# First loads on two queues, direct stacking and paired residual loads in a two-layer decoder trunk

## The chip, the cores and the metric

The kernel runs on one core of one Trainium2 chip. The metric is the device time of one execution in microseconds (us), as the median of several runs. The engines are TensorE (PE in the profile; PEld is its weight load), VectorE (DVE), ScalarE (ACT), GpSimd (POOL) and SyncE (SP, which here only issues DMAs). ACT and POOL can issue DMAs as well.

## The reference

Two pre-norm residual layers over 512 positions of width 2048, and a last normalisation. All sizes here are float32.

```python
for layer in range(2):
    h = rmsnorm(x, norm_g[layer])
    parts = split(h @ w_in[layer], 8)           # 8 parts of 256 columns
    if layer % 2 == 0:
        qa, ka, va, ga, qb, kb, vb, gb = parts
        oa = dilated_mixture(rope(heads(qa)), rope(heads(ka)), heads(va))
        ob = moba(rope(heads(qb)), rope(heads(kb)), heads(vb))
        y = concat(merge(oa) * silu(ga), merge(ob) * silu(gb))
    else:
        qc, kc, vc, gc, qd, kd, vd, gd = parts  # q and k of C in two halves of 32
        oc = diff_attention(rope(qc), rope(kc), heads(vc), lam, subln_g)
        od = stick_breaking(heads(qd), heads(kd), heads(vd))
        y = concat(merge(oc) * silu(gc), merge(od) * silu(gd))
    x = x + y @ w_out[layer]                    # y has 512 columns
return rmsnorm(x, final_norm_g)
```

Each of the four branches has 4 heads of 64.

## The kernel before

Every product is made from split operands. An operand a is rounded to a high part (type fp32r) on ACT, and DVE or POOL forms the low part, a minus the high part. A product is then three matmuls: high by high, low by high and high by low (`mm3`, L185). The activations lie transposed, 16 tiles of 128 features by 512 positions: HH and HL are the high and low parts of x times the gain.

The weights come in 80 units of 128x1024 (512 KB), 40 for each layer, in the order of use. `load_unit` (L142) loads a unit into one of three `raw` buffers, and `split_half` (L159) splits half a unit into whi and wlo, of which there are two buffers. `tick` (L178) is called once for each half unit of matmuls; it keeps the loads up to four units and the splits two half units ahead. All these loads stand in SP's queue, which works in program order, as every engine does.

A layer first makes the projections. In layer 0 the values V come first: `v_unit_half` (L314) runs 16 k tiles, each with 12 matmuls of 512 columns for the four blocks of 128 positions. Then 12 chunks of 128 columns (q, k and gates) are made. The work of the heads is put into this stream of matmuls at positions written out by hand (`SCHED`, L41). Chunks of q and k are rotated on DVE and stacked for the score matmuls: high and low parts of one head stand one above the other in the partitions of a tile st, so that one matmul sums several of the three products. For branch C of layer 1, with 32 rows for each half head, `stack4` (L366) does this with DMAs from tiles hi and lo.

The output projection (`outproj`, L635) has 16 chunks dc of 128 features. Each is made of four parts, one for each pair of heads (`part`, L627; 12 matmuls in all), added to the residual xr by `evac`, and in layer 0 written to DRAM as x1d. The first PRE chunks (2 in layer 0, 5 in layer 1) are opened before the last gate's y is there, with three parts each. `get_x` (L616) loads residuals three chunks ahead; in layer 1 into the four buffers of tag "prob", one tile of 512 columns in each buffer of 1280. The accumulators are PSUM banks of tags "acc" (2 banks) and "s" (3 banks). In layer 1 the projection makes 384 of the positions transposed, and `last` (L646) makes the other 128 in their natural layout, also after the projection; the residual is transposed on PE for these (L678). `after` (L657) takes squares for the last normalisation and multiplies by the last gain on ACT (L663); `scale_t` (L702) multiplies by the reciprocal root at the end.

At the start, `run` (L931) issues WARM matmuls of zeros, then the first loads on SP: xg (the first tile of x and the gain columns together), the two halves of unit 0, tile 1 of x, unit 1 and tiles 2 to 4 of x. The first tile's HH and HL are made on DVE (L240, L241).

Of the kernel before, what the change touches and what calls it, by code (L numbers as in the profile page):

```python
# [39 lines left out]
WARM = 8  # L40
# [42 lines left out]
class Body:  # L83
# [58 lines left out]
    def load_unit(self, part=0):  # L142
# [3 lines left out]
        if part == 2:  # L146
            self.nc.sync.dma_start(self.raw[0][:, 512:], self.a["w"][0][:, 512:])
            self.nload += 1
            return
        if part == 1:  # L150
            self.raw[0] = self.wp.tile([128, 1024], F32, tag="raw", bufs=3, name="raw")
            self.nc.sync.dma_start(self.raw[0][:, :512], self.a["w"][0][:, :512])
            return
        self.nload += 1
        t = self.wp.tile([128, 1024], F32, tag="raw", bufs=3, name="raw")
        self.nc.sync.dma_start(t, self.a["w"][u])
# [28 lines left out]
    def mm3(self, out, lh, ll, rh, rl, first, last):  # L185
        mm = self.nc.tensor.matmul
        mm(out, lhsT=lh, rhs=rh, start=first, stop=False)  # L187
        mm(out, lhsT=lh, rhs=rl, start=False, stop=False)  # L188
        mm(out, lhsT=ll, rhs=rh, start=False, stop=last)  # L189
# [44 lines left out]
    def make_h(self, x, l, kt, square=True, g=None):  # L234
        nc = self.nc
        if g is None:
            g = self.g[:, l, kt:kt + 1]
            nc.scalar.activation(self.HH[:, kt], x, AF.Copy, scale=g)
        else:
            nc.vector.tensor_scalar(self.HH[:, kt], x, g, None, op0=OP.mult)  # L240
# [14 lines left out]
    def load_x(self, src, kt, tag=None):  # L255
        if tag:
            x = self.ap.tile([128, 1280], F32, tag=tag, bufs=4, name="xr")[:, :S]
        else:
            x = self.tmp("xr")
        self.nc.sync.dma_start(x, src[kt])  # L260
        return x
# [52 lines left out]
    def v_unit_half(self, u, half, kt):  # L314
        h, l = self.whi[u], self.wlo[u]
        w = slice(512 * half, 512 * half + 512)
        if u == 0 and half == 0:
            for x, y in ((self.HH, h), (self.HL, h), (self.HH, l)):
                for t in range(NT):
                    self.nc.tensor.matmul(self.vps[t], lhsT=x[:, kt, 128 * t:128 * t + 128], rhs=y[:, w],  # L320
                                          start=x is self.HH and y is h, stop=False)
# [44 lines left out]
    def stack4(self, st, src, key):  # L366
# [693 lines left out]
```

## Time and profile before

| | us |
|---|---|
| median of 3 runs | 527.46 (527.19 to 529.7) |
| profiled execution | 527.0 |
| its span, first to last instruction | 524.9 |
| PE busy | 511.5 (97%) |
| DVE busy | 331.8 (63%) |
| ACT busy | 293.3 (56%) |
| POOL busy | 180.0 (34%) |

The profile is of one execution. The page gives busy times and groups; the timeline lists instructions in order of time, and what ended the idle time before one. Matmuls are pipelined: in the timeline a matmul's drawn duration overlaps the next one's.

### The profile page before, as it was taken

The numbers are of one execution on the slowest core, as the hardware profiler recorded it, in microseconds if no ns is written. First come the engines' busy times: TensorE is split into PE (matmuls) and PEld (weight loads), VectorE is DVE, ScalarE is ACT, GpSimd is POOL, SyncE is SP. The second block draws the span as 40 slices with busy tenths as digits, with TensorE's granted clock in tenths as the row PEclk, the third lists the DMA queues.
The fourth block names the chain that finished last, engine by engine and source line by source line (L and its number), as shares of the span: only waits on it lengthen the run. The fifth ranks groups of instructions, "written<-read, shape, count | busy, mean of one in ns | idle before, by whom it ended". The sixth has DMA issues, their size and how long they took to land.

```text
span 524.9 us, 7398 instructions
## 1 busy us (share of the span) xinstructions
PE 511.5 (97%) x2505; PEld 430.7 (82%) x2505; DVE 331.8 (63%) x678; ACT 293.3 (56%) x588; POOL 180.0 (34%) x171
## 2 busy tenths in 40 slices
PE   8999999999999999999999998999999999999993
PEld 5888888888888888788888887888888888898993
DVE  5545358787786755797862872564557856784444
ACT  5477244355436554566546464743446678857843
POOL 2304353304224023377403233114520322444841
PEclk9999999999999999999999999999999999999998
DMA  8895352244314223688534274232551313156717
GB/s 306 282 401 180 120 124 93 68 117 121 120 41 121 81 80 107 204 288 302 182 121 121 80 200 123 83 119 80 146 145 71 108 54 116 62 179 208 239 70 252
DMA packets 30374, 77.65 MB, mean 148 GB/s; under 512 B 4480, under 2 KB 7424, under 8 KB 29952
## 3 DMA queue, kind: packets, MB, share of 16 engines
q1 hardware_dynamic: 27264, 70.36, 39.3%
q0 software_dynamic: 2784, 6.29, 5.5%
q10 hardware_dynamic: 288, 0.52, 0.3%
q8 instruction: 20, 0.33, 0.3%
q14 instruction: 18, 0.15, 0.1%
HBM read 61.43 MB, written 8.39 MB: 133 GB/s over the span
## 4 chain that ended last, share of the span: by engine, by line
PE 91%; DMA 3%; ACT 2%; DVE 2%; issue 1%; POOL 0%; ACTq 0%; SPq 0%; POOLq 0%
PE acc L187 17%; PE acc L189 17%; PE acc L188 17%; PE oacc L188 5%; PE oacc L189 5%; PE oacc L187 5%; PE v L187 4%; PE v L189 4%; PE v L188 4%; PE ops L509 3%; PE pt L481 3%; PE s L415 2%; DMA st<-st 1%; PE z L532 1%; PE s L446 1%
## 5 line engine op out<-in xcount | busy, mean ns | idle before, releaser
L176 POOL TENSOR_TENSOR wlo<-raw,whi 128x512 fp32r<-128x512 f32 x67 | 90.7, 1359 | 192.3 <-ACT whi L174 146.9
L187 PE MATMUL acc<-hh,whi 128*128 128x512 f32 x384 | 154.2, 402 | 0.0
L189 PE MATMUL acc<-hh,wlo 128*128 128x512 f32 x384 | 150.1, 391 | 0.0
L188 PE MATMUL acc<-hl,whi 128*128 128x512 f32 x384 | 149.7, 390 | 0.0
L174 ACT ACTIVATE whi<-raw 128x512 fp32r<-128x512 f32 x148 | 90.5, 625 | 88.7 <-issue 42.7
L189 PEld LDWEIGHTS acc<-hh,wlo 128*128 128x128 f32 x384 | 72.1, 188 | 15.6
L188 PEld LDWEIGHTS acc<-hl,whi 128*128 128x128 f32 x384 | 72.3, 188 | 12.9
L187 PEld LDWEIGHTS acc<-hh,whi 128*128 128x128 f32 x384 | 72.3, 188 | 12.7
L176 DVE TENSOR_TENSOR wlo<-raw,whi 128x512 fp32r<-128x512 f32 x81 | 59.2, 737 | 29.4 <-ACT whi L174 26.9
L187 PE MATMUL v<-whi,hh 128*128 128x512 f32 x124 | 48.4, 390 | 0.0
L189 PE MATMUL v<-whi,hl 128*128 128x512 f32 x124 | 48.3, 389 | 0.0
L188 PE MATMUL v<-wlo,hh 128*128 128x512 f32 x124 | 48.2, 389 | 0.0
L395 ACT ACTIVATE prob<-prob,m 128x512 f32<-128x512 f32 (+3 forms) x56 | 29.7, 552 | 28.3 <-DVE m L392 28.3
L487 DVE TENSOR_TENSOR pt<-pt 128x384 fp32r<-128x384 f32 (+1 forms) x48 | 27.4, 598 | 22.2 <-ACT pt L486 22.1
L486 ACT ACTIVATE pt<-pt 128x384 fp32r<-128x384 f32 (+1 forms) x48 | 23.5, 524 | 27.2 <-PE pt L481 26.9
L187 PE MATMUL oacc<-y,whi 128*128 128x512 f32 (+1 forms) x80 | 30.9, 386 | 0.1
L188 PE MATMUL oacc<-y,whi 128*128 128x512 f32 (+1 forms) x80 | 30.4, 380 | 0.2 <-DVE y L577 0.2
L189 PE MATMUL oacc<-y,wlo 128*128 128x512 f32 (+1 forms) x80 | 30.3, 378 | 0.0
L189 PEld LDWEIGHTS v<-whi,hl 128*128 128x128 f32 x124 | 23.3, 188 | 4.9
L188 PEld LDWEIGHTS v<-wlo,hh 128*128 128x128 f32 x124 | 23.3, 188 | 4.7
L187 PEld LDWEIGHTS v<-whi,hh 128*128 128x128 f32 x124 | 23.3, 188 | 4.6
L253 POOL TENSOR_TENSOR ss<-ss,sq 128x512 f32<-128x512 f32 x15 | 21.8, 1451 | 11.2 <-ACT sq L249 11.1
(219 smaller groups left out, 836.8 us busy)
## 6 DMA issues: line engine op xcount, KB each, us to landing
raw<-w SPq DMA_DIRECT2D x79, 512.0 KB, 3.4
xr<-xt SPq DMA_DIRECT2D x31, 256.0 KB, 4.4
xnat<-xnat SPq DMA_DIRECT2D x8, 512.0 KB, 7.5
x1d<-x SPq DMA_DIRECT2D x16, 256.0 KB, 2.8
xr<-x1d SPq DMA_DIRECT2D x16, 256.0 KB, 3.5
st<-st POOLq DMA_DIRECT2D x24, 128.0 KB, 3.5
out_t_dram<-x2a SPq DMA_DIRECT2D x10, 192.0 KB, 2.8
out_t_dram<-x2b SPq DMA_DIRECT2D x6, 192.0 KB, 2.5
```

The costliest lines, as they stand in the source:

```text
L174: self.nc.scalar.activation(h, t, AF.Copy)
L176: eng.tensor_tensor(l, t, h.bitcast(F32), op=OP.subtract)
L187: mm(out, lhsT=lh, rhs=rh, start=first, stop=False)
L188: mm(out, lhsT=lh, rhs=rl, start=False, stop=False)
L189: mm(out, lhsT=ll, rhs=rh, start=False, stop=last)
L253: nc.gpsimd.tensor_tensor(ss, ss, sq, op=OP.add)
L395: nc.scalar.activation(p, p, AF.Exp, bias=m[:, t:t + 1], scale=-1.0, **kw)
L415: nc.tensor.matmul(out, lhsT=Q()[:, 2 * i + arr, 128 * t:128 * t + 128], rhs=Q()[:, 4 + i, :n], start=arr == 0, stop=arr == 1)
L481: nc.tensor.transpose(bank[:, col + 128 * (t - c):col + 128 * (t - c) + 128], st["p"][:, QOFF[t] + 128 * c:QOFF[t] + 128 * c + 128], self. ...
L486: nc.scalar.activation(h, src, AF.Copy)
L487: nc.vector.tensor_tensor(l, src, h.bitcast(F32), op=OP.subtract)
L509: nc.tensor.matmul(b[:, 128 * c:], lhsT=self.V[:, c, vh], rhs=st[k][:, OFF[c]:OFF[c] + WID[c]], start=c == 0 and k == "h", stop=c == NT - ...
```

## The change

At the start, the first half of unit 0 is issued from ACT's queue, and xg is cut in two, half of the first tile with the gains first. ACT issues unit 1, unit 2 and tiles 2 to 4 of x between its first splits. The first tile's HH and HL are made in halves, and the first twelve matmuls go through the first two position blocks before the others. There are seven warm matmuls in place of eight. In `stack4` every copy is made straight from hi and lo: eight transfers of 64 KB on SP and eight on POOL, where four and four were followed by copies from the stacked tile to itself. In the output projections, the two first chunks do the two matmuls that don't need the last gate's low part before the third; in layer 0 the chunks 2 to 4 also take banks of tag "s". In layer 1 residuals are loaded in pairs. The last gain of chunks 0 to 4 moves from ACT into the final scaling.

```diff
-WARM = 8
+WARM = 7
...
-    def load_unit(self, part=0):
+    def load_unit(self, part=0, eng=None):
...
-        self.nc.sync.dma_start(t, self.a["w"][u])
+        (eng or self.nc.sync).dma_start(t, self.a["w"][u])
...
+    def mm3(self, out, lh, ll, rh, rl, first, last, which=3):
         mm = self.nc.tensor.matmul
+        if which == 3:
+            mm(out, lhsT=lh, rhs=rh, start=first, stop=False)
+            mm(out, lhsT=lh, rhs=rl, start=False, stop=False)
+            mm(out, lhsT=ll, rhs=rh, start=False, stop=last)
+        elif which == 2:
+            mm(out, lhsT=lh, rhs=rh, start=first, stop=False)
+            mm(out, lhsT=ll, rhs=rh, start=False, stop=False)
+        else:
+            mm(out, lhsT=lh, rhs=rl, start=False, stop=last)
...
+    def make_h0(self, i):
+        nc = self.nc
+        o = i * (S // 2 + 3 * KT)
+        x, g = self.xg[:, o:o + S // 2], self.xg[:, S // 2:S // 2 + 1]
+        w = slice(S // 2 * i, S // 2 * i + S // 2)
+        nc.vector.tensor_scalar(self.HH[:, 0, w], x, g, None, op0=OP.mult)
+        nc.vector.scalar_tensor_tensor(self.HL[:, 0, w], x, g, self.HH[:, 0, w].bitcast(F32),
+                                       op0=OP.mult, op1=OP.subtract)
...
         if u == 0 and half == 0:
-            for x, y in ((self.HH, h), (self.HL, h), (self.HH, l)):
-                for t in range(NT):
+            for x, y, t in [(x, y, t) for ts in ((0, 1), (2, 3))
+                            for x, y in ((self.HH, h), (self.HL, h), (self.HH, l)) for t in ts]:
...
+        hrows, lrows = ((0, 96), (32, 64)) if key else ((0, 64), (32, 96))
         for i in range(4):
             p = slice(32 * i, 32 * i + 32)
-            nc.sync.dma_start(sf[0:32, z + i], hi[p])
-            nc.gpsimd.dma_start(sf[32:64, z + i], lo[p])
-        if key:
-            nc.gpsimd.dma_start(sf[64:96, z:z + 4], sf[32:64, z:z + 4])
-            nc.gpsimd.dma_start(sf[96:128, z:z + 4], sf[0:32, z:z + 4])
-        else:
-            nc.gpsimd.dma_start(sf[64:128, z:z + 4], sf[0:64, z:z + 4])
+            for k in range(2):
+                nc.sync.dma_start(sf[hrows[k]:hrows[k] + 32, z + i], hi[p])
+                nc.gpsimd.dma_start(sf[lrows[k]:lrows[k] + 32, z + i], lo[p])
...
+    def get_pair(self, k):
+        if k < KT // 2:
+            t = self.ap.tile([128, 1280], F32, tag="prob", bufs=4, name="xr")[:, :2 * S]
+            t = t.rearrange("p (k s) -> p k s", k=2)
+            self.nc.sync.dma_start(t, self.px[2 * k:2 * k + 2].rearrange("k p s -> p k s"))
+            self.xs[2 * k], self.xs[2 * k + 1] = t[:, 0], t[:, 1]
...
             for k in range(3):
-                self.get_x(k)
-        self.accs[dc] = self.bank("acc" if dc < 2 or dc >= PRE[self.pl] else "s", "oacc")[:, :self.pw]
+                self.get_pair(k) if self.pl else self.get_x(k)
+        self.accs[dc] = self.bank("s" if 2 <= dc < 5 else "acc", "oacc")[:, :self.pw]
...
         for dc in range(KT):
-            self.get_x(dc + 3)
-            if dc < PRE[self.pl]:
+            if not self.pl:
+                self.get_x(dc + 3)
+            elif dc % 2 == 0:
+                self.get_pair(dc // 2 + 3)
+            if dc < 2:
+                if dc == 0:
+                    self.part(0, 3, 2)
+                    self.part(1, 3, 2)
+                self.part(dc, 3, 1)
+            elif dc < PRE[self.pl]:
                 self.part(dc, 3)
...
-            nc.scalar.activation(X[dc], X[dc], AF.Copy, scale=self.g[:, 2, dc:dc + 1])
+            if dc >= PRE[1]:
+                nc.scalar.activation(X[dc], X[dc], AF.Copy, scale=self.g[:, 2, dc:dc + 1])
...
-                eng.tensor_tensor(X[dc], X[dc], r, op=OP.mult)
+                if dc < PRE[1]:
+                    eng.scalar_tensor_tensor(X[dc], X[dc], self.g[:, 2, dc:dc + 1], r, op0=OP.mult, op1=OP.mult)
+                else:
+                    eng.tensor_tensor(X[dc], X[dc], r, op=OP.mult)
...
                 if kt == 0:
-                    self.make_h(self.x0.pop(0), 0, 0, False, self.xg[:, S:S + 1])
+                    q = self.nc.scalar
+                    self.make_h0(0)
                     self.split_half()
+                    self.load_unit(0, q)
+                    self.x0[2] = self.load_x(self.a["xt"], 2, q)
+                    self.make_h0(1)
                     self.split_half()
                     self.make_h(self.x0.pop(1), 0, 1, False)
+                    for k in (3, 4):
+                        self.x0[k] = self.load_x(self.a["xt"], k, q)
+                    self.load_unit(0, q)
...
-        nc.sync.dma_start(self.xg, self.a["xg"])
-        self.x0[0] = self.xg[:, :S]
+        c = S // 2 + 3 * KT
+        nc.sync.dma_start(self.xg[:, :c], self.a["xg"][:, :c])
+        self.load_unit(1, nc.scalar)
+        nc.sync.dma_start(self.xg[:, c:], self.a["xg"][:, c:])
         nc.scalar.preload_act_table_set("exp_and_others")
-        self.load_unit(1)
-        self.load_unit(2)
+        self.load_unit(2, nc.sync)
         self.x0[1] = self.load_x(self.a["xt"], 1)
-        nc.gpsimd.tensor_copy(self.g.rearrange("p a b -> p (a b)"), self.xg[:, S:])
-        self.load_unit()
-        for kt in range(2, 5):
-            self.x0[kt] = self.load_x(self.a["xt"], kt)
+        nc.gpsimd.tensor_copy(self.g.rearrange("p a b -> p (a b)"), self.xg[:, S // 2:c])
```

## Rows read from the trace of the kernel before

**Rows 1.** The page, part 1: busy time, share of the span and instructions.

```profile
PE 511.5 (97%) x2505; PEld 430.7 (82%) x2505; DVE 331.8 (63%) x678; ACT 293.3 (56%) x588; POOL 180.0 (34%) x171
```

**Rows 2.** What PE waited for: total us, times, longest.

```profile
PE s L446 <- DMA st<-st: 1.6, 1, 1.6
...
PE xnp L678 <- DMA xr<-x1d: 0.9, 1, 0.9
```

**Rows 3.** Timeline, start: begin us, duration us, engine, line, operation, count [idle before <-releaser].

```profile
0.74 0.38 SPq L941 DMA_DIRECT2D xg<-xg  x1
...
1.18 0.42 SPq L152 DMA_DIRECT2D raw<-w  x1
...
1.19 3.48 PE L938 MATMUL warm<-zero 128*128 128x512 bf16 x8 [1.19 <-DVE zero L935]
...
3.55 0.53 DVE L240 TENSOR_SCALAR hh<-xg 128x512 fp32r<-128x512 f32 x1 [2.42 <-DMA xg<-xg]
...
4.57 0.63 ACT L174 ACTIVATE whi<-raw 128x512 fp32r<-128x512 f32 x1 [2.55 <-DMA raw<-w]
...
5.25 1.19 PE L320 MATMUL v<-whi,hh 128*128 128x512 f32 x4 [0.58 <-ACT whi L174]
```

**Rows 4.** Timeline, the k tiles behind the first; last, a DMA issue on ACT.

```profile
7.39 0.75 DVE L241 SCALAR_TENSOR_TENSOR hl<-xr,gcols,hh 128x512 fp32r<-128x512 f32 x1 [0.35 <-ACT hh L238]
...
8.03 0.63 ACT L174 ACTIVATE whi<-raw 128x512 fp32r<-128x512 f32 x1 [0.68 <-DMA raw<-w]
8.11 0.39 PE L187 MATMUL v<-whi,hh 128*128 128x512 f32 x1
...
9.45 0.75 DVE L241 SCALAR_TENSOR_TENSOR hl<-xr,gcols,hh 128x512 fp32r<-128x512 f32 x1
9.47 0.39 PE L187 MATMUL v<-whi,hh 128*128 128x512 f32 x1
...
519.12 0.41 ACTq L804 DMA_DIRECT2D out_n_dram<-nat  x1
```

**Rows 5.** Timeline, PE and DVE, where the first output projection closes its first chunks.

```profile
213.98 0.51 PE L187 MATMUL oacc<-y,whi 128*128 128x512 f32 x1
214.70 0.50 PE L188 MATMUL oacc<-y,whi 128*128 128x512 f32 x1 [0.22 <-DVE y L577]
...
215.47 1.39 DVE L958 TENSOR_TENSOR x<-oacc,xr 128x512 f32<-128x512 f32 x2 [0.82 <-PE oacc L189]
...
215.74 0.39 PE L189 MATMUL oacc<-y,wlo 128*128 128x512 f32 x1
216.21 0.50 PE L187 MATMUL oacc<-y,whi 128*128 128x512 f32 x1
...
217.03 0.40 PE L187 MATMUL oacc<-y,whi 128*128 128x512 f32 x1
```

**Rows 6.** Timeline, the second stacking of layer 1 and the scores behind it.

```profile
308.67 2.78 SPq L375 DMA_DIRECT2D st<-hi  x4
...
309.66 1.98 POOL L376 DMA_DIRECT2D st<-lo  x4 [1.96 <-DVE lo L372]
...
319.48 0.63 ACT L174 ACTIVATE whi<-raw 128x512 fp32r<-128x512 f32 x1 [2.89 <-PE v L189]
...
323.02 0.88 PE L446 MATMUL s<-st 128*128 128x512 f32 x4 [1.59 <-DMA st<-st]
```

**Rows 7.** The chain that ended last: begin us, us, what (a DMA until its landing).

```profile
311.14 3.21 DMA st<-lo
...
315.49 7.18 DMA st<-st
...
475.43 2.60 DMA xr<-x1d
```

**Rows 8.** Timeline: a gain on ACT in the second projection; DVE in the tail.

```profile
475.96 0.62 ACT L663 ACTIVATE x2a<-x2a,gcols 128x384 f32<-128x384 f32 x1
...
510.13 0.69 DVE L715 TENSOR_TENSOR nat<-nacc,nat 128x512 f32<-128x512 f32 x1 [0.28 <-PE nacc L189]
```

More of the change, by code (lines that the diff above doesn't have):

```diff
@@ L146, in load_unit @@
         if part == 2:
-            self.nc.sync.dma_start(self.raw[0][:, 512:], self.a["w"][0][:, 512:])
+            eng.dma_start(self.raw[0][:, 512:], self.a["w"][0][:, 512:])
             self.nload += 1
@@ L151, in load_unit @@
             self.raw[0] = self.wp.tile([128, 1024], F32, tag="raw", bufs=3, name="raw")
-            self.nc.sync.dma_start(self.raw[0][:, :512], self.a["w"][0][:, :512])
+            eng.dma_start(self.raw[0][:, :512], self.a["w"][0][:, :512])
             return
@@ L183, in tick @@
         self.gh += 1
-    def mm3(self, out, lh, ll, rh, rl, first, last):
+    def mm3(self, out, lh, ll, rh, rl, first, last, which=3):
         mm = self.nc.tensor.matmul
-        mm(out, lhsT=lh, rhs=rh, start=first, stop=False)
-        mm(out, lhsT=lh, rhs=rl, start=False, stop=False)
-        mm(out, lhsT=ll, rhs=rh, start=False, stop=last)
+        if which == 3:
[7 more added lines that the diff above has]
+            mm(out, lhsT=lh, rhs=rl, start=False, stop=last)
     def rstd(self, ss, n, mul, add=None, eng=None):
@@ L253, in square, with load_x @@
             nc.gpsimd.tensor_tensor(ss, ss, sq, op=OP.add)
[L255 to L260, printed above, removed]
+    def load_x(self, src, kt, eng=None):
+        x = self.tmp("xr")
+        (eng or self.nc.sync).dma_start(x, src[kt])
         return x
@@ L317, in v_unit_half @@
         if u == 0 and half == 0:
-            for x, y in ((self.HH, h), (self.HL, h), (self.HH, l)):
-                for t in range(NT):
-                    self.nc.tensor.matmul(self.vps[t], lhsT=x[:, kt, 128 * t:128 * t + 128], rhs=y[:, w],
-                                          start=x is self.HH and y is h, stop=False)
+            for x, y, t in [(x, y, t) for ts in ((0, 1), (2, 3))
+                            for x, y in ((self.HH, h), (self.HL, h), (self.HH, l)) for t in ts]:
+                self.nc.tensor.matmul(self.vps[t], lhsT=x[:, kt, 128 * t:128 * t + 128], rhs=y[:, w],
+                                      start=x is self.HH and y is h, stop=False)
             return
@@ L623, in open_dc, with part @@
             for k in range(3):
-                self.get_x(k)
-        self.accs[dc] = self.bank("acc" if dc < 2 or dc >= PRE[self.pl] else "s", "oacc")[:, :self.pw]
-    def part(self, dc, j):
+                self.get_pair(k) if self.pl else self.get_x(k)
+        self.accs[dc] = self.bank("s" if 2 <= dc < 5 else "acc", "oacc")[:, :self.pw]
+    def part(self, dc, j, which=3):
         u, k = self.pl * UNITS + 32 + dc // 2, dc % 2
@@ L632, in part @@
         self.mm3(self.accs[dc], h[:, e], lo[:, e], self.YH[:, e, :self.pw], self.YL[:, e, :self.pw],
-                 j == 0, j == 3)
+                 j == 0, j == 3, which)
     def outproj(self, evac):
         for dc in range(KT):
-            self.get_x(dc + 3)
-            if dc < PRE[self.pl]:
+            if not self.pl:
[8 more added lines that the diff above has]
+            elif dc < PRE[self.pl]:
                 self.part(dc, 3)
```

14 lines of the change are left out of this document (6 added, 8 removed).

## The prediction, made before the change was built or run

> **What bounds the kernel now.** I read the page first: PE is busy 97% of the span [rows 1], so no other engine is the bound over any long stretch, and what an edit can win is the time in which PE stands still. Then the list of what PE waited for [rows 2]: it has few entries, and the two on DMAs name one place each. Then, in PE's timeline, the starts of the matmuls. The reader has to know one thing of that view: a 128x512 matmul is drawn 0.39 us long, but the next starts earlier: from 8.11 to 9.47 are six undisturbed steps [rows 4], so 0.227 us each. So an idle time g in the view is a loss of about g + 0.16 us, and a loss is best read from starts. I went through all starts in that way. Beside some 90 ns after each run of transposes, PE loses time in four places: the start, the first output projection, the first s of layer 1 and the second output projection. The change touches all four. After the last matmul stands a tail of DVE, ACT and stores, which it hardly touches.
>
> **The start.** The first real matmul starts at 5.25; it waits for the split on ACT (4.57 to 5.20), which waits for the first half of the first weight tile, issued on SP at 1.18, behind xg at 0.74 [rows 3]. The change issues this half on ACT's queue, so at 0.74, and cuts xg: 152 KB go ahead, 128 KB behind. The landing of two transfers issued at the same time on two queues is not in this trace. Early end: as xg alone, 280 KB from 0.74 to 3.55 [rows 3], so 3.55 instead of 4.55, a gain of 1.0; the seven warm matmuls, 3.48/8 = 0.43 each [rows 3], then end near 4.2 and no longer fit much gain than that. Late end: the two queues share and the half lands as before, gain 0. I take 0.5, in the middle and near the 0.44 us by which the issue comes earlier. The Trainium skill, "DMA: Bandwidth & Descriptors", section "Issuing engines are not separate DMA queues", speaks against more: transfers from several engines interleave on the same DMA engines and a second issuer saves its issue time alone. By it the term would be 0.44; this trace, with one queue in use there, doesn't show it. The half-width HH and HL on DVE (0.53 in full width [rows 3]) come before the split ends, and the new order of the first twelve matmuls needs only these halves for its first six, so they don't set the start.
>
> What is then late next? PE has twelve matmuls per k tile, 2.86 us for the first [rows 3, 4]. The second k tile would start at 4.75 + 2.86 = 7.6 and needs HL of x1 two steps later, at 8.06; it was ready at 7.39 + 0.75 = 8.14 [rows 4]. With the same bytes ahead of x1, a wait of 0.1 at most remains. For the third k tile, ACT now issues five loads among its first splits, 0.41 each [rows 4]: two before the second split, where ACT waited for data anyway, and three, 1.2 us, ahead of the split that stood at 8.03. ACT was idle 0.68 there, so split and HH come about 0.5 later, and PE wants them 0.5 earlier. HL of x2 ended at 9.45 + 0.75 = 10.20, and was wanted at 8.11 + 2.72 + 0.45 = 11.28: of a margin of 1.1, 0.1 is left. So the supply is at the edge but holds; if raw 1 and raw 2, now issued 2 to 3 us later, share the DMA engines with raw 3 and x5 of SP, I bound the loss at 0.8. Range of the start: -0.3 to +1.0, value 0.5.
>
> **The first output projection.** Two chunks stand ready but for the last gate. The first of their last three matmuls starts at 213.98, the second waits for the low part of y (214.70), and the third chunk waits at 215.74 to 216.21 for a PSUM bank, because DVE empties the first chunk only from 215.47 [rows 5]. From 213.98 to 217.03 are nine steps; undisturbed they take 9 x 0.227 = 2.04, here they took 3.05: 1.0 lost. After the change four matmuls that don't need the low part come first, 4 x 0.227 = 0.91, so the low part is wanted at 214.89 and is there at 214.70; chunks 2 to 4 take banks of tag "s", free since the attention heads. Chunks 5 and 6 take "acc" again, over 8 us of PE after these are emptied. Gain 1.0; what could be late next is DVE's evacuation, twelve matmuls (2.7 us) per 0.70 us of DVE. Lower bound 0.6 (the bank alone late), upper 1.0.
>
> **Direct stacking.** For each of four chunks of layer 1, the split halves go from hi and lo to the stacked tile. Before, four 64 KB transfers on SP and four on POOL, then POOL waits for these to land and issues one or two copies of 256 or 512 KB from the tile to itself. The last such copy takes 7.18 us, to 322.67 [rows 7], and s starts at 323.02 after 1.59 us of idle: a loss of 1.75 [rows 6]. After: eight on each queue, the same bytes, no second stage. SP: 308.67 + 8 x 2.78/4 = 314.2; POOL: 309.66 + 8 x 1.98/4 = 313.6 [rows 6]. With the 3.21 us that a first-stage transfer took [rows 7], the last lands near 317.4; even with the 7.18 of the copies it is 321.4, when PE is there at 321.28. So the whole 1.75 is won; lower bound 1.6. What is queued behind: on SP four more issues, 2.8 us, stand before the next weight load (311.55 before). The split that uses that load (319.48) waited for PE, not for the load [rows 6], and it is made at least two half units ahead of its use, 24 matmuls or 5.4 us: the delay is hidden; without that cover it would cost up to 1. On POOL the queue gets free sooner than before (313.6, where the last copy was issued from 315.49 on [rows 7]), so splits behind it gain. The other three stackings had no loss and have none to win.
>
> **Residual pairs.** In the second output projection the fifth residual tile was issued at 475.43, since the four buffers were full until the first chunk was emptied, and landed 2.60 later [rows 7]; PE was idle 0.9 [rows 2], a loss of 0.9 + 0.16, some 1.0. After, a buffer holds two tiles: three pairs are asked for where three tiles were, the fourth pair where the fourth tile was, so tiles 0 to 7 are there before PE reaches the fifth chunk. The same bytes; half the issues on SP. Gain 1.0. What is late next there is ACT: squares, gains and splits follow each other closely, 0.62 us for each gain [rows 8]. The change takes five of these off ACT (chunks 0 to 4, 3.1 us), more than PE gains, so the splits keep their lead. Lower bound 0.5.
>
> **The gains moved to the end.** The five are multiplied in on DVE in the final scaling: a two-operand instruction becomes a three-operand one. Such a pair stands at 0.69 [rows 8] and 0.75 [rows 4] for 512 columns: 0.05 for 384, 0.2 for the first four. They stand before DVE's wait of 0.28 for PE [rows 8], which hides them; uncovered they cost 0.25.
>
> **Sum.** 0.5 + 1.0 + 1.75 + 1.0 = 4.25. The profiled execution took 527.0 (span 524.9 and 2.1 around it), so 522.8. The median of the runs is 527.46, 0.46 more, and gives 523.2. I forecast 523.0. With all terms at their lower ends (-0.3, 0.6, 1.6, 0.5; and 0.25 lost in the tail) the gain is 2.2, the time 525.3 from the median; with all at the upper ends 4.75, 522.3 from the profiled execution.
>
> **Rivals.** (a) The start gives nothing or takes some back: shared DMA engines, or ACT's issues making the third to fifth k tile late. For it: margins of 0.1. Against: each of these was ahead by 1 us before. It gives 523.5 to 524.3. (b) One of the inner stalls is only replaced: s still waits because raw loads and sixteen small transfers share the engines, or the second projection becomes bound by ACT's splits. For: the copies took 7.18 where the first stage took 3.2, so transfers there did get in each other's way. Against: the margins above. It costs 1.0 to 1.75 of the sum: 524.0 to 525.0. (c) Slower than before: TensorE's clock. The warm matmuls run at 0.43 per 512 columns, the 1.2 GHz level; the first real ones, after 0.58 us idle, at 0.23, the 2.4 GHz level [rows 3, 4]. One warm matmul fewer could leave the lower level standing when the real ones begin; each then costs 0.2 more. From 22 such matmuls on (22 x 0.2 = 4.4) it eats the whole sum, from 35 on the kernel is over 0.5% slower, and 40 of them give 523.2 + 8 = 531. Against: the idle time before the first real matmul is about as long as before, so activity hardly changes. The Trainium skill, "TensorE: Matmul & The Clock Gate", Part 1, adds that the moment of release shifts from run to run; one trace can't show that.
>
> **How the numbers follow.** Forecast 0.69, (a) 0.14, (b) 0.12, (c) 0.05. Half a per cent, 2.6 us, is about what a measurement of this kernel can tell from no change: faster means below 524.8. The forecast lies there, but not with every term at its low end; with (a) that is 0.81. Most of (b) at its worst, such a forecast at its low end and (c) in a mild form (20 to 35 matmuls) give same, 0.15; slower 0.04. Range 521.9 to 525.3: up to the sum of the low ends, which takes in (a) and (b) whole; down to the upper ends and 0.4 below, since the lowest run before is 0.3 under the median.
>
> **What would show it.** First real matmul near 4.75 at 0.23 steps; no PE wait on DMA st or xr; nine steps in 2.05 us where the first projection closes; s near 319.8 (323.02 less 0.5, 1.0 and 1.75), with no idle. It would be wrong if PE's gaps among the first five k tiles add up to over 0.5, if the first real matmuls are 0.43 apart, or if s still shows a wait.

## The result, and the profile of the changed kernel

| us | before | after |
|---|---|---|
| median of the runs on the same chip | 528.37 (527.19 to 529.7) | 523.7 (522.72 to 525.54) |
| profiled execution | 527.0 | 524.88 |
| its span | 524.9 | 522.7 |

The ratio is 0.9921, with an interval of 0.9901 to 0.9942: the changed kernel takes 0.8% less time, clear of the interval. The same kernel on another chip gave 0.994 (0.992 to 0.9959), a median of 524.74 (523.11 to 525.47). The 527.46 that the prediction set out from was the median of the first three of the seven runs before. Ratios are worked out over all runs and differ by up to 0.15% from the quotient of the medians. Two runs of the experiments, one of e7 (574.19 us) and one of e10 (2946.32 us), were far slower than all others of their kernels and are left out of medians and ratios. The two profiled executions are only 2.1 us apart, because the one before was faster than all seven timed runs and the one after was the second slowest of its seven. So the profiles can't be subtracted as totals; each stage is read from the starts of its matmuls.

Part 1 of the page (busy us, share of the span, instructions) answers [rows 1]:

```profile
PE 511.6 (98%) x2504; PEld 431.1 (82%) x2504; DVE 335.7 (64%) x680; ACT 289.8 (55%) x583; POOL 187.2 (36%) x181
```

What PE waited for in the changed kernel (line, releaser, us in total, times, longest), beside [rows 2]:

```profile
PE warm L970 <- DVE zero L967: 1.2, 1, 1.2
PE v L188 <- ACT hh L252: 0.6, 1, 0.6
PE v L189 <- POOL wlo L176: 0.2, 1, 0.2
```

Both waits on DMAs, st and xr, are gone, and so is the one on the split in front of the first real matmul (0.58 in [rows 3]; in e12, the same kernel, it was there again with 0.49). Two are new, and both stand in the fifth k tile of the start. The first is on ACT's hh, the second on POOL's wlo.

The start, in PE's timeline of the changed kernel (start, us, engine, line, operation, tiles, count, and in brackets idle time before it with what ended it), beside [rows 3]:

```profile
1.19 3.17 PE L970 MATMUL warm<-zero 128*128 128x512 bf16 x7 [1.19 <-DVE zero L967]
4.51 1.22 PE L329 MATMUL v<-whi,hh 128*128 128x512 f32 x2
5.53 0.86 PE L329 MATMUL v<-whi,hl 128*128 128x512 f32 x2
6.23 0.62 PE L329 MATMUL v<-wlo,hh 128*128 128x512 f32 x2
...
8.05 0.39 PE L188 MATMUL v<-whi,hh 128*128 128x512 f32 x1
```

The first real matmul starts at 4.51 instead of 5.25. But two matmuls take 1.02 (4.51 to 5.53), the next two 0.70, and only from 6.23 on 0.46. Twelve undisturbed steps are 2.72, so the second k tile could have started at 4.51 + 2.72 = 7.23. It starts at 8.05: 0.82 are lost without any idle time, and the second k tile is only 0.06 ahead of that before.

Then the fifth k tile, in the timeline of ACT, POOL and PE:

```profile
15.71 0.63 ACT L174 ACTIVATE whi<-raw 128x512 fp32r<-128x512 f32 x1 [4.28 <-DMA raw<-w]
...
16.25 0.70 ACT L252 ACTIVATE hh<-xr,gcols 128x512 fp32r<-128x512 f32 x1
16.42 1.28 POOL L176 TENSOR_TENSOR wlo<-raw,whi 128x512 fp32r<-128x512 f32 x1 [4.19 <-ACT whi L174]
...
17.01 0.51 PE L188 MATMUL v<-whi,hh 128*128 128x512 f32 x1 [0.59 <-ACT hh L252]
...
17.75 0.49 PE L189 MATMUL v<-wlo,hh 128*128 128x512 f32 x1 [0.24 <-POOL wlo L176]
```

ACT stands idle 4.28 us for a weight load; its split comes at 15.71, its hh at 16.25, and PE waits. The chain of waits that leads there names the load (start, us, what):

```profile
7.56 8.04 DMA raw<-w
```

This is unit 2. ACT issued it at 7.56, as the last of its five loads, and it took 8.04 us to land. Before, in the timeline of SP and ACT:

```profile
4.56 2.83 SPq L156 DMA_DIRECT2D raw<-w  x2
...
11.38 0.63 ACT L174 ACTIVATE whi<-raw 128x512 fp32r<-128x512 f32 x1 [0.83 <-DMA raw<-w]
```

The first of SP's two loads is unit 2: it was issued at 4.56, took 6.7 us to land, and ACT split it from 11.38 on. So of the 4.3 us by which the split now comes later, 3.0 are the later issue and 1.3 the longer landing. The sixth k tile now starts at 20.70 instead of 18.99: at that point the changed kernel is 1.71 us behind. Everything that it wins, it wins later.

The first output projection in PE's timeline, beside [rows 5]:

```profile
215.69 0.50 PE L192 MATMUL oacc<-y,whi 128*128 128x512 f32 x1
216.03 0.39 PE L193 MATMUL oacc<-y,wlo 128*128 128x512 f32 x1
...
216.72 0.63 PE L195 MATMUL oacc<-y,whi 128*128 128x512 f32 x2
217.19 0.39 PE L188 MATMUL oacc<-y,whi 128*128 128x512 f32 x1
```

From 215.69 on, the four matmuls that don't need the low part of y, then the two that do (L195), then the third chunk (217.19). No idle time is left. One step is 0.34 long, the others 0.23.

The stacking of layer 1 beside [rows 6] and [rows 7]: issues on SP and POOL in the timeline, then the table of DMA issues for the stretch from 308 to 323 (KB each, median us to landing), then PE's timeline.

```profile
309.46 5.19 SPq L386 DMA_DIRECT2D st<-hi  x8
...
314.76 1.09 SPq L156 DMA_DIRECT2D raw<-w  x2
...
310.45 3.91 POOL L387 DMA_DIRECT2D st<-lo  x8 [3.51 <-DVE lo L381]
```

```profile
st<-hi SPq DMA_DIRECT2D x8, 64.0 KB, 2.7
st<-lo POOLq DMA_DIRECT2D x8, 64.0 KB, 2.6
```

```profile
321.85 0.39 PE L190 MATMUL v<-whi,hl 128*128 128x512 f32 x1
322.07 0.79 PE L452 MATMUL s<-st 128*128 128x512 f32 x4
```

The last of the eight on SP is issued by 314.65 and lands some 2.7 later; s starts at 322.07, one step after the matmul before it. The copies of the tile to itself, 7.18 us for the last, have left the chain.

The transposes of the fourth and the fifth residual tile in the second projection, in PE's timeline, first before, then after, beside [rows 2] and [rows 7]:

```profile
476.52 0.27 PE L678 MATMUL xnp<-ident,xr 128*128 128x128 f32 x1
...
478.17 0.30 PE L678 MATMUL xnp<-ident,xr 128*128 128x128 f32 x1 [0.86 <-DMA xr<-x1d]
```

```profile
475.39 0.27 PE L700 MATMUL xnp<-ident,xr 128*128 128x128 f32 x1
...
476.02 0.27 PE L700 MATMUL xnp<-ident,xr 128*128 128x128 f32 x1
```

From the fourth to the fifth it was 1.65 and is 0.63; none of the transposes waits any more. And DVE's tail, first before, then after, beside [rows 8]:

```profile
507.90 1.95 DVE L705 TENSOR_TENSOR x2a<-x2a,rep 128x384 f32<-128x384 f32 x4 [0.16 <-ACT R L297]
```

```profile
505.71 2.19 DVE L728 SCALAR_TENSOR_TENSOR x2a<-x2a,gcols,rep 128x384 f32<-128x384 f32 x4 [0.16 <-ACT R L306]
507.95 0.69 DVE L740 TENSOR_TENSOR nat<-nacc,nat 128x512 f32<-128x512 f32 x1
```

The four scalings take 2.19 instead of 1.95, and DVE's wait of 0.28 for PE behind them is gone: the gains cost DVE 0.24, near the 0.2 put in the prediction for the first four, and the end nothing.

From starts at fixed places, the stages of the profiled executions (us, changed kernel less the kernel before): start, to the sixth k tile, +1.71; first projection -0.91; stacking -1.75; second projection -1.06, and another -0.17 between s and its beginning, whose cause was not looked for; tail -0.08. The span: -2.26.

### The profile page after: what moved, and what is told of

Read it like the earlier page. It is cut to its first block, busy times and chain, and to the rows that moved or that the text cites. A ratio compares the mean times of both kernels' runs of the same rounds, so it can differ in the third digit from the quotient of the medians.

```text
span 522.7 us, 7398 instructions
## 1 busy us (share of the span) xinstructions
PE 511.6 (98%) x2504; PEld 431.1 (82%) x2504; DVE 335.7 (64%) x680; ACT 289.8 (55%) x583; POOL 187.2 (36%) x181
## 3 DMA queue, kind: packets, MB, share of 16 engines
q0 software_dynamic: 2944, 5.25, 4.5%
## 4 chain that ended last, share of the span: by engine, by line
PE 94%; DMA 3%; ACT 1%; DVE 1%; SPq 0%; issue 0%; ACTq 0%
PE acc L188 17%; PE acc L190 17%; PE acc L189 17%; PE v L190 5%; PE v L188 5%; PE v L189 5%; PE oacc L188 5%; PE oacc L190 5%; PE oacc L189 5%; PE ops L515 4%; PE pt L487 3%; PE s L421 2%; DMA raw<-w 2%; PE z L538 1%; PE s L452 1%; DMA xr<-xt 1%
## 5 line engine op out<-in xcount | busy, mean ns | idle before, releaser
L190 PEld LDWEIGHTS acc<-hh,wlo 128*128 128x128 f32 x384 | 72.1, 188 | 15.6
L176 DVE TENSOR_TENSOR wlo<-raw,whi 128x512 fp32r<-128x512 f32 x81 | 61.4, 764 | 30.2 <-ACT whi L174 29.5
L188 PE MATMUL oacc<-y,whi 128*128 128x512 f32 (+1 forms) x76 | 29.1, 383 | 0.0
L190 PE MATMUL oacc<-y,wlo 128*128 128x512 f32 (+1 forms) x76 | 28.8, 379 | 0.0
L189 PE MATMUL oacc<-y,whi 128*128 128x512 f32 (+1 forms) x76 | 28.8, 379 | 0.0
L265 POOL TENSOR_TENSOR ss<-ss,sq 128x512 f32<-128x512 f32 x15 | 23.5, 1567 | 8.5 <-ACT sq L261 8.4
```

The costliest lines, as they stand in the source:

```text
L176: eng.tensor_tensor(l, t, h.bitcast(F32), op=OP.subtract)
L265: nc.gpsimd.tensor_tensor(ss, ss, sq, op=OP.add)
```

## The experiments

The questions were where the start's gain had gone, and whether the three inner parts stand on their own. All kernels compute the whole reference. The table gives the median of the runs and the ratio to the kernel before on the same chip (so "before" has one median for each of the four chips), and three places of the one profiled execution; e10 and e11 stand in the text alone. "Lost in k tile 1" is the start of the second k tile less that of the first real matmul less 2.72; "lost to k tile 6" is the start of the sixth less that of the second less 10.88 (four k tiles of 2.72). In e7 a wait of 0.2 for hh is part of the first of these; the second, in e7 and in e3, falls in the second k tile, not in the fifth.

| kernel | median us | ratio (interval) | first real matmul | lost in k tile 1 | lost to k tile 6 | span |
|---|---|---|---|---|---|---|
| before | 526.95 to 528.37 | 1 | 5.25 | 0.14 | 0 | 524.9 |
| after | 523.7 | 0.9921 (0.9901 to 0.9942) | 4.51 | 0.82 | 1.77 | 522.7 |
| after, again (e12) | 524.74 | 0.994 (0.992 to 0.9959) | 4.85 | 1.93 | 0 | 522.4 |
| inner parts alone (e1) | 523.9 | 0.993 (0.9906 to 0.9955) | 5.49 | 0.15 | 0 | 521.4 |
| start alone (e2) | 527.62 | 1.0023 (1.0 to 1.0045) | 4.92 | 0.14 | 0.51 | 525.7 |
| later loads on SP (e3) | 524.61 | 0.9942 (0.9921 to 0.9964) | 4.84 | 0.38 | 0.10 | 520.9 |
| 8 warm (e4) | 523.62 | 0.9929 (0.9907 to 0.9951) | 4.90 | 0.18 | 0.47 | 521.2 |
| unit 2 first (e8) | 525.32 | 0.9956 (0.9938 to 0.9973) | 4.91 | 0.18 | 2.88 | 523.6 |
| SP and 8 warm (e9) | 523.87 | 0.9935 (0.9909 to 0.9961) | 4.99 | 0.50 | 0 | 521.2 |
| SP and 9 warm (e13) | 523.89 | 0.9933 (0.9909 to 0.9957) | 4.93 | 0.31 | 0.02 | 520.9 |
| start before, 10 warm (e14) | 524.14 | 0.9945 (0.9925 to 0.9964) | 5.63 | 0.67 | 0 | 522.0 |
| start before, gains on ACT (e7) | 524.86 | 0.9956 (0.9938 to 0.9974) | 4.94 | 0.60 | 0.46 | 522.7 |

**e1, the inner parts alone.** The changed kernel with the start of the kernel before.

```diff
-WARM = 7
+WARM = 8
...
-        self.load_unit(1, nc.scalar)
+        self.load_unit(1)
...
+        self.load_unit()
+        for kt in range(2, 5):
+            self.x0[kt] = self.load_x(self.a["xt"], kt)
```

> The start of the kernel before (one queue, eight warm matmuls, whole first tile); stacking, first projection, pairs and gains as changed. Theory A (what the two profiles read: the inner parts win 0.9 + 1.75 + 1.1 = 3.8 us, and the changed start costs 1.7): 3.8 us faster than before, so about 524.6 against 528.4, and in the profile the same start as before (first real matmul 5.25, fifth k tile at 16.3 to 16.5), no wait of PE on st or xr. It is then faster than the changed kernel by up to 1.7. Theory B (the profiled execution had a bad start, and the changed start gains 0.5 to 0.9 in most executions, as the medians 528.37 and 523.70 would have it): also 3.8 faster than before, but about 0.9 slower than the changed kernel.

Measured: against the kernel before, the start +0.25, the first projection -0.90, the stacking -1.75, span 521.4 (-3.57). So the gain is had without the changed start; the ratio, 0.993, is that of the whole change within its interval, and 0.7% of 527.12 is 3.7 us, near the 3.8 of both theories; against the changed kernel neither A's gain of up to 1.7 nor B's loss of 0.9 shows. The first real matmul, at 5.49, shows that the start of before moves too: 5.25 was one execution.

**e2, the start alone.** The kernel before with the changed start; `mm3`, `stack4`, the projections and the gains as they were.

```diff
-            for k in range(2):
-                nc.sync.dma_start(sf[hrows[k]:hrows[k] + 32, z + i], hi[p])
-                nc.gpsimd.dma_start(sf[lrows[k]:lrows[k] + 32, z + i], lo[p])
+            nc.sync.dma_start(sf[0:32, z + i], hi[p])
+            nc.gpsimd.dma_start(sf[32:64, z + i], lo[p])
...
-                self.get_pair(k) if self.pl else self.get_x(k)
+                self.get_x(k)
...
-            if dc >= PRE[1]:
+            if True:
```

> Only the start is changed (queues, halves, order of the first twelve matmuls, seven warm matmuls); the inner parts are those of before. Theory A: 1.7 us slower than before, with PE waiting about 1.7 in the fifth k tile for unit 2 and tile 4 of x, which land 8 and 6.5 us after their issue beside unit 3 and tiles 5 and 6 from SP. Theory B: 0.5 to 0.9 faster than before, without that wait. Both: the three inner waits are there again (s on st 1.6, xnp on xr 0.9).

Measured: 1.0023 (1.0 to 1.0045), no gain. The first real matmul and the second k tile are 0.33 ahead, but at the sixth k tile the kernel is 0.18 behind: again ACT waits for unit 2 (3.48 us), and the fifth k tile loses 0.51. The waits for st and xr stand in its list as before (1.8 and 1.1). Neither theory had the size: the time is 1.2 longer by the ratio, between the 1.7 longer of A and the 0.5 to 0.9 shorter of B. The wait in the fifth k tile belongs to the start, not to the inner parts.

**e3, the later loads on SP in order.** Only the first half of unit 0 stays on ACT's queue.

```diff
-                    self.load_unit(0, q)
-                    self.x0[2] = self.load_x(self.a["xt"], 2, q)
                     self.make_h0(1)
...
-                    for k in (3, 4):
-                        self.x0[k] = self.load_x(self.a["xt"], k, q)
-                    self.load_unit(0, q)
...
+        self.load_unit()
+        for kt in range(2, 5):
+            self.x0[kt] = self.load_x(self.a["xt"], kt)
```

> The changed kernel, but ACT issues only the first half of unit 0; unit 1, tiles 2 to 4 of x and unit 2 are issued by SP, right behind tile 1, as before. Theory A (unit 2 is late because ACT issues it behind its first work, at 7.56 in place of 4.56, and shares the DMA engines with what SP issues at the same time): no wait in the fifth k tile, the first real matmul still near 4.5, so 0.3 to 0.7 ahead of before at the sixth k tile and some 2 us ahead of the changed kernel's profile; about 4.3 us faster than before. Theory B: within 0.5 us of the changed kernel's median.

Measured: the wait of the fifth k tile is gone. ACT's split of unit 2 in its timeline:

```profile
11.34 0.63 ACT L174 ACTIVATE whi<-raw 128x512 fp32r<-128x512 f32 x1 [0.85 <-DMA raw<-w]
```

It comes at 11.34 where it came at 15.71. Two things are put back at once here: SP issues unit 2 at 4.53, 3.0 earlier than ACT did, and all loads but the first are in one queue. The table of DMA issues of the first 9.5 us (KB each, median us to landing), first that of the changed kernel, then that of e3:

```profile
raw<-w ACTq DMA_DIRECT2D x2, 512.0 KB, 6.6
xr<-xt SPq DMA_DIRECT2D x3, 256.0 KB, 8.1
xr<-xt ACTq DMA_DIRECT2D x3, 256.0 KB, 5.3
raw<-w SPq DMA_DIRECT2D x1, 512.0 KB, 6.6
```

```profile
xr<-xt SPq DMA_DIRECT2D x6, 256.0 KB, 5.8
raw<-w SPq DMA_DIRECT2D x3, 512.0 KB, 5.6
```

In one queue the median for a 512 KB load is 5.6 us (unit 2 itself takes 6.7, as in the kernel before) and for a tile of x 5.8. In two queues ACT's two weight loads took 5.1 and 8.04 (the 6.6 of the table is the middle of these), SP's unit 3 took 6.6, its tiles of x 8.1 and ACT's 5.3. Between 5 and 10 us the DMA engines moved 293 GB/s in the changed kernel and 388 in e3 and in the kernel before. So the supply of these loads is the cause of the wait. How much of it is the later issue and how much the second queue, e3 doesn't separate; unit 2's own times put 3.0 of the 4.3 us on the issue. The sixth k tile of e3 starts at 18.92, 1.78 earlier than in the changed kernel, and the span is 1.7 shorter. But the first real matmul stood at 4.84, not near 4.5, and the time is 3.1 us under the kernel before by the ratio, not 4.3: the runs lie from 523.09 to 525.64, and the profiled one is among the fastest of them.

**e4, eight warm matmuls.** The changed kernel with the eighth back.

```diff
-WARM = 7
+WARM = 8
```

> The changed kernel with eight warm matmuls. In the changed kernel's profile the first four real matmuls were some 0.43 to 0.6 apart. If the missing warm matmul keeps TensorE at 1.2 GHz (theory C): the first real matmuls run 0.23 apart, up to 0.7 us won. If the moment of release is not set by the eighth one: the low level lasts as long as in the changed kernel, and the time is within 0.5 us of it, with the first real matmul at 4.6 to 4.7 at the earliest (the eighth one ends there).

Measured: the matmuls of the first k tile run at 0.23, and 0.18 is lost there, not 0.82. The wait for unit 2 is in it too, but smaller (0.47 to the sixth k tile). The median is 523.62. Taken alone this would make the missing eighth matmul the cause; e2, with seven and 0.14 lost, and e9 to e14 below contradict it.

**e8, unit 2 first on ACT's queue.** Was it late because two tiles of x stand before it, or because SP's loads run beside it? Here it is issued ahead of tiles 3 and 4.

```diff
+                    self.load_unit(0, q)
                     for k in (3, 4):
                         self.x0[k] = self.load_x(self.a["xt"], k, q)
-                    self.load_unit(0, q)
```

> The changed kernel, but ACT issues unit 2 ahead of tiles 3 and 4 of x. In the profiles of the changed start, unit 2 (issued 6.9 to 7.6) landed at 14.0 to 15.6 and PE lost 0.4 to 1.7 in the fifth k tile. Theory A1 (the order on ACT's queue decides): unit 2 lands by 12.5, the wait in the fifth k tile goes, but tile 3 lands some 1.3 later and may cost up to 0.5 in the fourth. Theory A2 (the bytes that SP issues at the same moment decide: unit 3, tiles 5 and 6): unit 2 still lands after 13 and the wait shrinks by less than half.

Measured: unit 2, issued at 5.98, took 7.3 us and so was there at 13.3, earlier than the 15.6 of the changed kernel but after 13, as A2 has it. Now tile 3 is late. ACT's and PE's timelines, and the table of issues:

```profile
14.90 0.72 ACT L252 ACTIVATE hh<-xr,gcols 128x512 fp32r<-128x512 f32 x1 [4.62 <-DMA xr<-xt]
```

```profile
15.67 0.50 PE L188 MATMUL v<-whi,hh 128*128 128x512 f32 x1 [2.26 <-ACT hh L252]
```

```profile
xr<-xt SPq DMA_DIRECT2D x3, 256.0 KB, 8.0
xr<-xt ACTq DMA_DIRECT2D x3, 256.0 KB, 8.5
```

PE waits 2.26 in the fourth k tile, where A1 put 0.5 at most, and 2.88 are lost up to the sixth. The order within ACT's queue only chooses which load is late. That the two queues slow each other, the later loads of SP taking their share while ACT's urgent ones are under way, fits e3 and e8 both; but no run changes this alone, with the issue times kept, so it is argued and not shown.

**e10, the fourth unit held back.** SP should issue unit 3 two half units later, with the third k tile, so that less runs beside ACT's loads.

```diff
-        while self.nload < min(self.gh // 2 + 4, 2 * UNITS):
+        while self.nload < min(self.gh // 2 + (4 if self.gh > 1 else 3), 2 * UNITS):
```

> The changed kernel, but SP issues unit 3 only with the third k tile's tick, not the first's. Theory A2 (sharing): with 512 KB less beside it, unit 2 lands by 12.7 (about 1.3 earlier, 512 KB at the 390 KB/us that this start moves), and the fifth k tile has no wait. Theory A1 (order): unit 2 lands at 14 or later as before. Time: within 0.5 us of the changed kernel in both, since the wait is 0.4 in most executions; up to 1.7 better where it was large.

Measured: a median of 525.0, ratio 0.9949 (0.993 to 0.9969), no better than the changed kernel. It didn't separate anything: SP isn't held by PE's progress, so taking unit 3 back in the order of the program let SP issue tiles 5 and 6 at 4.04 and 5.28 and unit 3 at 7.02 all the same. The same loads run beside ACT's. These three times are from the one profile of e10, the run of 2946 us, in which the matmuls alone are slow (last section).

**e9, e13 and e14: how many warm matmuls?** e9 and e13 have e3's loads with `WARM = 8` and `WARM = 9`; e14 has e1's start with `WARM = 10`, so that PE is never idle before the first real matmul.

For e9 against e3, and e14 against e1:

```diff
-WARM = 7
+WARM = 8
...
-WARM = 8
+WARM = 10
```

> The changed kernel with only the first half of unit 0 on ACT and the other loads on SP, and eight warm matmuls. The same with seven gave 523.1 to 525.6, in two heaps, while both kernels with eight warm matmuls and the inner parts kept within 1.1 us (523.1 to 524.4). Theory C (with seven, the clock's release comes late in a part of the executions): the runs keep within 1.2 us, median near 523.2, and the first real matmuls are 0.23 apart. Rival: the spread is of the loads' order; then it stays over 2 us.

> The changed kernel with only the first half of unit 0 on ACT, the other loads on SP, and nine warm matmuls, so that PE stands idle at most 0.1 us between the last warm and the first real matmul (some 0.6 with seven). So far the 1.2 GHz level lasted until 4.3 to 8.7 us after the span's start in the profiles, with seven or eight alike. Theory D (an idle PE ahead of the first real matmul puts the release off): the first real matmuls, at about 5.0, run 0.23 apart, the sixth k tile starts at 18.8 to 19.0, the runs keep within 1.2 us, and the median is at or under 523.5, some 3.9 to 4.3 faster than before. Rival (the release comes when it comes): the spread stays near 2 us, and the median within 0.5 of that with eight.

> The start of before with ten warm matmuls in place of eight, inner parts as changed: the last warm one ends near 5.5, when the first half of unit 0 is split, so PE isn't idle. Theory D: up to 0.2 later at the first real matmul, but never a real matmul at 1.2 GHz; runs within 1 us, median 0 to 0.5 faster than with eight (3.2 to 3.7 faster than before). Rival: the same time as with eight, or 0.2 slower.

Measured: e9 lost 0.50 in the first k tile, more than e3 with seven warm matmuls (0.38); e13 lost 0.31; e14 lost 0.67. PE's timeline of e14:

```profile
1.19 4.45 PE L957 MATMUL warm<-zero 128*128 128x512 bf16 x10 [1.19 <-DVE zero L954]
5.63 1.73 PE L323 MATMUL v<-whi,hh 128*128 128x512 f32 x4
7.20 1.08 PE L323 MATMUL v<-whi,hl 128*128 128x512 f32 x4
```

There is no idle time from 1.19 on, and still the first four real matmuls take 1.57 where four steps are 0.91: theory D's "never a real matmul at 1.2 GHz" failed. In e13 the first pair took 0.74 where two steps are 0.45, and in e9 the runs spread over 1.9 us, not 1.2. Neither more warm matmuls nor less idle time made the slow steps go. All medians lie between 523.87 and 524.14.

**e12, the changed kernel again.** Nothing is edited; it ran on the chip of e8 to e10.

> The changed kernel itself, on the same chip as the three above, so that these are compared with it and not only with before. Theory A (its start is worth nothing on the average: up to 0.7 earlier, and 0.4 to 1.7 lost in the fifth k tile): 3.2 to 3.8 us faster than before, not the 4.7 of its first measurement, with a spread of about 2.5 us. Theory B (its start gains in most executions): 4.3 to 4.7 faster.

Measured, in PE's timeline:

```profile
4.85 1.22 PE L329 MATMUL v<-whi,hh 128*128 128x512 f32 x2 [0.49 <-ACT whi L174]
5.87 1.05 PE L329 MATMUL v<-whi,hl 128*128 128x512 f32 x2
...
8.43 0.77 PE L329 MATMUL v<-whi,hl 128*128 128x512 f32 x2
...
9.50 0.39 PE L188 MATMUL v<-whi,hh 128*128 128x512 f32 x1
```

With the same code, the first eight real matmuls take 3.58 (4.85 to 8.43), 0.45 each, the step of the warm ones (3.17/7 = 0.45, the 1.2 GHz level), and 1.93 are lost in the first k tile instead of 0.82. The wait for unit 2 doesn't appear, since PE now comes too late to notice it: theory A's time came, 3.2 us under the kernel before by the ratio, but by another way. So the moment at which the step falls to 0.23 differs between executions of one kernel, and one profile for each of e4, e9 and e13 can't tell what a warm matmul is worth.

**e7, pairs without the move of the gains.** e1 with the five last gains on ACT, as before.

```diff
-            if dc >= PRE[1]:
+            if True:
                 nc.scalar.activation(X[dc], X[dc], AF.Copy, scale=self.g[:, 2, dc:dc + 1])
...
-                if dc < PRE[1]:
+                if False:
```

> The start of before, inner parts as changed, but the five gains stay on ACT in the second projection. Prediction's step (the gains on DVE keep ACT ahead of PE; without them ACT has 3.1 us more there, and splits come late): PE loses up to 1 us between chunks 6 and 10, and 0.2 is won in the tail on DVE; 0.3 to 0.8 slower than with the gains moved. Rival (ACT has enough room, the move is for nothing): no gap of PE there, the same time within 0.2.

Measured: the residual tiles are there in time, but PE waits elsewhere. The timelines of ACT, DVE and PE:

```profile
478.34 0.62 ACT L174 ACTIVATE wkh<-raw 128x512 fp32r<-128x512 f32 x1
```

```profile
478.99 0.69 DVE L176 TENSOR_TENSOR wkl<-raw,wkh 128x512 fp32r<-128x512 f32 x1 [3.25 <-DMA xr<-x1d]
479.60 0.55 DVE L683 TENSOR_TENSOR x2a<-oacc,xr 128x384 f32<-128x384 f32 x1
```

```profile
480.29 0.41 PE L188 MATMUL oacc<-y,wkh 128*128 128x384 f32 x1 [0.62 <-DVE x2a L683]
```

ACT's split (478.34) stands behind a gain; DVE's low part (478.99) waits for the split, which ends at 478.96 (its row names a residual load, but that one landed 1.4 earlier); DVE's evacuation (479.60) stands behind the low part; PE waits 0.62 for the bank. From the sixth k tile to the first nacc matmul the kernel is 0.98 slower than e1: the pairs' gain is all but spent. The move of the gains isn't a side edit, it is what lets the pairs pay.

**e11, the banks alone.** The kernel before, with chunks 2 to 4 of the first projection in the banks of tag "s".

```diff
-        self.accs[dc] = self.bank("acc" if dc < 2 or dc >= PRE[self.pl] else "s", "oacc")[:, :self.pw]
+        self.accs[dc] = self.bank("s" if 2 <= dc < 5 else "acc", "oacc")[:, :self.pw]
```

> Before, with the one edit that chunks 2 to 4 of the first projection take banks of tag s. Prediction's step: of the 1.0 lost there, the bank's part (0.36) goes and the wait for the low part of y (0.6) stays: nine steps from the first matmul of part 3 take 2.65 us in place of 3.05. Rival (one wait hides the other): both go or none.

Measured (526.29 us, its only run): the first projection -0.41, the wait for the bank gone, that for the low part of y left, in PE's timeline:

```profile
214.42 0.50 PE L187 MATMUL oacc<-y,whi 128*128 128x512 f32 x1
215.15 0.51 PE L188 MATMUL oacc<-y,whi 128*128 128x512 f32 x1 [0.23 <-DVE y L577]
```

So the 0.91 splits into 0.41 for the banks and, by subtraction, 0.50 for the order of the matmuls, which was not run alone.

## Why the prediction was right, and where it was not

The time, 523.7, lies 0.7 above the forecast of 523.0 and in the range. The sum behind it was right in its inner terms and wrong in its start.

- **What bounds the kernel.** PE's idle time was the place to look: all four places named changed, and nothing else did by over 0.2. e1 and e2 share the gain out: the inner parts alone have it, the start alone has none.
- **First projection, 1.0:** measured 0.91 in the changed kernel and 0.88 to 0.91 in every kernel with both edits. The 0.09 short are mostly a step of 0.34 in front of the second matmul. The lower bound of 0.6 was worked out for the bank alone late; e11 gives the banks 0.41, so 0.50 would have been left.
- **Stacking, 1.75:** measured 1.75 in all of these kernels. The last transfer, put near 317.4, is issued by 314.65 with a median of 2.7 to landing. The four more issues on SP held no one up. What one trace couldn't show is that the stall itself varies: measured in the same way, the two kernels that keep the old stacking lost 0.63 (e11) and 1.95 (e2). So 1.75 is what the profile before lost, not what every execution does.
- **Pairs, 1.0:** 1.06, by the step named. That ACT would be late next unless the five gains moved was stated, and e7 shows it with 0.98.
- **Gains on DVE, 0:** right, hidden behind the 0.28 as said.
- **Start, +0.5 (-0.3 to +1.0): the step that failed.** Its first half held in the main: the first real matmul is 0.74 earlier in the profile, and in the eight profiles with the first load on ACT (e10's left out) it stands at 4.51 to 4.99, in the five with the start of before at 4.94 to 5.67; the means, 4.86 and 5.40, are 0.54 apart. Its second half, that the supply "is at the edge but holds" and that a loss is bounded at 0.8, did not hold. Two mechanisms took the gain back, and both stood among the rivals. The first is rival (a), and it was mis-sized. The margins that were worked out, up to the third k tile, did hold: the third and the fourth start at 10.77 and 13.54 and are 0.05 late together. For the fifth k tile there was no sum behind the 0.8. Unit 2, named as issued 2 to 3 us later, came 3.0 later and took 8.04 to land in place of 6.7; the fifth k tile lost 1.77 in the profile and 0.5 in e2 and e4, and e8 lost 2.88 by another order. With these loads back on SP, e3 lost 0.10. Rival (c) came, but small: 0.82 are lost in the profile and 1.93 in e12, where 0.14 are lost in any case; at 0.2 for each slow matmul these are some three and nine, and the mild form of (c) had 20 to 35. Its cause as told, one warm matmul fewer, isn't shown: e14, with ten and without a gap, lost 0.67, and e2, with seven, 0.14.
- **The signs.** Two of the three signs of being wrong came, both in the start: PE stands idle for 0.59 and 0.24 in the fifth k tile, over the 0.5, and the first real matmuls are 0.51 apart. The third didn't: s shows no wait. Nine steps at the end of the first projection take 2.18, near the 2.05, and s starts at 322.07 and not near 319.8, which is the start's 2.2 (1.71 behind in place of 0.5 ahead).

In the profile the start thus cost 1.71. Over the runs it was worth about nothing: the changed kernel against e1, which has all but the start, stands at 0.9921 and 0.994 to 0.993, and e2 is at 1.0023. That the forecast still came near follows from the sizes. The inner terms were 3.75 of the 4.25, they and the small shifts beside them measure 3.97, and e1, which has them alone, stands 0.7% (3.7 us by the ratio) under the kernel before. The start's 0.5 is less than the width of any interval here: the two measurements of the changed kernel, 0.79% and 0.6% (4.2 and 3.2 us), lie on both sides of e1. That the first of them came within 0.7 us of the forecast is in part luck: the other, 524.74, is 1.7 above it.

The Trainium skill, "DMA: Bandwidth & Descriptors", section "Issuing engines are not separate DMA queues", says that transfers of several issuing engines interleave on the same DMA engines. The medians of e3 (5.6 and 5.8 us) beside those of the changed kernel and e8 (up to 8.5) agree with that, though the later issue has its part in them. Its other half, that a second issuer saves its issue time, held for the first load only, which went out at 0.74 in place of 1.18; unit 2 went out 3.0 later.

What stays open: why the step of the first real matmuls falls to 0.23 at such different moments; how the supply's loss divides into later issue and shared DMA engines; and whether unit 2 could be in time with ACT issuing it while SP's later loads are held back, which e10 was meant to try and didn't. No kernel beat the changed one beyond its interval; the best medians are 523.62 (e4), 523.7 (after) and 523.87 (e9).

## What to carry to other kernels

A stall that is read from matmul starts and has its releaser beside it can be priced to a tenth of a us, but check what is late next: the residual pairs paid (1.06 us, against 0.08 in e7) only because five instructions left the engine whose splits came next. A second issuing engine brought only the first load forward here: the later ones had to wait for that engine's own work (unit 2 went out 3.0 us later), and then ran beside what the first queue had issued meanwhile. So work out the margin of each later consumer from both its issue and its landing; landings here were up to half as long again as in one queue. What happens in the first 10 us differs between executions of one kernel (the second k tile of the changed kernel started at 8.05 and at 9.50), so an edit of the start wants repeated timed runs, and one profile of it proves little.

## What the runs showed of the hardware

- The first slow steps end at no fixed moment. The first warm matmul starts at 1.19 or 1.20 in all kernels. The step had gone from 0.43 to 0.23 by the first real matmuls in some (0.14 lost in e2 and before), and only after eight of them in e12. The granted clock's column reads 1.00 in both stretches; the step is what shows the level.
- With loads of 256 and 512 KB in two queues at the same time the medians to landing spread from 4.0 (e2) to 8.5 us (e8), against 5.6 to 5.8 for the same loads in one queue (e3). Across queues the order of issue doesn't settle which lands first: in the changed kernel unit 3, issued on SP at 7.34, took 6.6, and unit 2, issued on ACT at 7.56, took 8.04.
- One execution of e10 took 2946 us, and its profile is that one. Its matmuls start some 1.2 us apart throughout (2504 of them in a span of 2944 us; for one pair of 512 columns 25.95 and 27.23), at a granted clock that is recorded as 1.00, while ACT, DVE and POOL are busy for 298.1, 328.9 and 178.6 us, much as in the other profiles. The cause is open.
